# Latent attention beside the out-projection, regrouped from one head every four steps to two heads every eight

## The chip, the core and the metric

The kernel runs on one core of a Trainium2 chip. The metric is the device time of one execution in microseconds, the median of three runs. The profile is of one further execution; its times are in microseconds from the first instruction of the span.

## The reference, cut to what matters

One decoder layer over 256 tokens and 2048 channels, in float32: a pooling mixer, latent attention of 8 heads and cross attention of 4 heads to a memory run side by side, their outputs are joined and projected, and a gated feed-forward follows. The change touches the causal attention of the latent heads and its place beside the product with `w_o`:

```python
s = jnp.einsum('bqhd,bkhd->bhqk', qblk, k).astype(jnp.float32) * scale
s = jnp.where(mask[None, None], s, -jnp.inf)
pr = jax.nn.softmax(s, axis=-1).astype(v.dtype)
return jnp.einsum('bhqk,bkhd->bqhd', pr, v)
...
x = x + jnp.concatenate([y_pool, y_mla, y_mem], axis=-1) @ w_o[l]
```

## The kernel before

Every large product is done with operands split in two: a high part, a ScalarE cast (`split_w`, L103, tile `wh`), and a low part, a VectorE subtraction (L104, tile `wl`), and TensorE multiplies high by high, low by high and high by low (L185 to L187). Four pairs of `wh` and `wl` buffers rotate, so a cast waits until TensorE has finished with the buffer four casts earlier.

The out-projection is cut into parts. A part loads 128 x 2048 weights and does four **steps**: a step is one call of `gemm_n` with one row of weights, on two blocks of tokens with three products each, so 6 matmuls of 128 x 512. Two steps share one `wh`/`wl` pair. After each of the first 36 steps `mla_steps` is called, and `done[0]` counts these calls; "step 18" below is the place behind the 18th step. The first half of the input channels (pooling and memory heads) comes first; the latent heads are multiplied only in the second half, head 0 in step 33, head 4 in step 37, head 7 in step 40.

A latent head has three pieces of work on TensorE:

- `scores`: 6 matmuls into a bank of PSUM (`psa`), the last of each block of rows adds the causal mask (L823). Softmax follows on VectorE (L521, L522, L526, L528) and ScalarE (L524) and leaves the tile `p`.
- `turn`: three 128 x 128 transposes of `p` into a bank (L534), copied by ScalarE to `pT` (L537).
- `values`: two products of `pT` with the values (L542, L544) into a bank, whose 256 columns `split_act` turns into a high and a low part of `cat`: a ScalarE cast (L194) and a VectorE subtraction (L195), both reading the bank.

`psa` is a pool of four banks of 128 x 512 float32 that rotate. Head 0 and 1 have their scores at step 3. From step 6 on, every fourth step does `values` of head h-1, `turn` of head h and `scores` of head h+2, and step 36 does the last `values`. Matmuls and transposes in `keep(...)` stay in the order in which the code issues them; ScalarE and VectorE work and the matmuls after step 36 are placed by a scheduler when the program is built. Between them VectorE also prepares sums of the weights of the last product (`job_sums`, L610, tile `wk`) and adds finished sums to the residual (L886, tile `x1n`).

Of the kernel before, what the change touches and what calls it, by code (L numbers as in the profile page):

```python
# [18 lines left out]
P = 128  # L19
T = 256  # L20
# [3 lines left out]
H = 8  # L24
# [41 lines left out]
def layer(ctx, tc, xT_d, xn_d, memT_d, vec_d, tab_d, w_z_d, w_mqkr_d, w_q_d, w_kv_d, w_mem_d, w_pool_d, w_o_d,  # L66
          w_g_d, w_u_d, w_dn_d, out_d):
    nc = tc.nc
# [8 lines left out]
    def nm(s):  # L77
        uid[0] += 1
        return f"{s}_{uid[0]}"

    def ps_main():
        return psm.tile([P, 512], F32, tag="m", name=nm("psm"))

    def ps_aux():
        return psa.tile([P, 512], F32, tag="a", name=nm("psa"))
# [7 lines left out]
    def keep(ins, on=True):  # L93

        return tc.keep_in_program_order(ins) if on else ins
# [93 lines left out]
    def split_act(dst, src, scale=None, kept=False):  # L189


        h, l = (dst[:, 0], dst[:, 1]) if len(dst.shape) == 3 else (dst[:, 0:T], dst[:, T:2 * T])
        if scale is None:
            nc.scalar.copy(h, src)  # L194
            nc.vector.tensor_tensor(l, src, h.bitcast(F32), op=ALU.subtract)  # L195
        else:
            keep(nc.scalar.activation(h, src, AF.Copy, scale=scale), kept)
            keep(nc.vector.scalar_tensor_tensor(l, src, scale, h.bitcast(F32), op0=ALU.mult, op1=ALU.subtract), kept)
# [118 lines left out]
    ps = ps_aux()  # L317
# [40 lines left out]
    for c in range(KD // 2):  # L358
# [13 lines left out]
        if c % 2:  # L372
            h = slice(2 * c - 2, 2 * c + 2)
# [5 lines left out]
    ps = ps_aux()  # L379
# [126 lines left out]
    class Head:  # L506
# [5 lines left out]
            self.blocks = [(k, i) for k in range(2) for i, (a, b) in enumerate(spans) if b - a > k * P]  # L512

        def score(self):
            ps = ps_aux()
            self.scores(ps)
            p = self.p = mp.tile([P, 512], F32, tag="p", name=nm("p"), bufs=2)
            st = mp.tile([P, 8], F32, tag="st", name=nm("st"), bufs=4)
            n = len(self.spans)
            for i, (a, b) in enumerate(self.spans):  # L520
                nc.vector.tensor_reduce(st[:, i:i + 1], ps[:, a:b], axis=AX.X, op=ALU.max, negate=True)  # L521
            nc.vector.tensor_tensor(st[:, 2:2 + n], st[:, 0:n], self.f, op=ALU.mult)  # L522
            for i, (a, b) in enumerate(self.spans):
                nc.scalar.activation(p[:, a:b], ps[:, a:b], AF.Exp, bias=st[:, 2 + i:3 + i], scale=self.f[:, i:i + 1],  # L524
                                     accum_out=st[:, 4 + i:5 + i])
            nc.vector.reciprocal(st[:, 6:6 + n], st[:, 4:4 + n])  # L526
            for i, (a, b) in enumerate(self.spans):
                nc.vector.tensor_scalar(p[:, a:b], p[:, a:b], st[:, 6 + i:7 + i], None, op0=ALU.mult)  # L528
# [7 lines left out]
            nb = len(self.blocks) * P  # L536
            nc.scalar.copy(self.pT[:, :nb], tp[:, :nb])  # L537

        def values(self):
            nb = len(self.blocks) * P  # L540
            o = ps_aux()
            keep(nc.tensor.matmul(o[:, 0:T], self.v_of(0), self.pT[:, 0:T], start=True, stop=False,  # L542
                                  skip_group_check=True))
            keep(nc.tensor.matmul(o[:, 2 * T - nb:T] if nb < 2 * T else o[:, 0:T], self.v_of(1), self.pT[:, T:nb],  # L544
                                  start=False, stop=True, skip_group_check=True))
            split_act(self.dst, o[:, 0:T])

    class MemHead(Head):
# [70 lines left out]
    for m in range(6):  # L619
        raw = load_w(w_z_d[m], STG)  # L620
        ps = ps_main()[:, 0:T]
# [52 lines left out]
    def pool_out():  # L674
        for a in range(2):
            ps = ps_aux()
            for g in (2 * a, 2 * a + 1):
                keep(nc.tensor.matmul(ps[:, (g % 2) * T:(g % 2 + 1) * T], wp[:, g * P:(g + 1) * P], zp[:, g, :],
                                      start=True, stop=True))
            for g in (2 * a, 2 * a + 1):  # L680
                split_act(cat[:, g, :], ps[:, (g % 2) * T:(g % 2 + 1) * T], v("pool_scale", g))
# [119 lines left out]
    def rope_keys():  # L801
        for tt in range(NT):
            t = tok()
            nc.vector.tensor_tensor(t[:].rearrange("p (h d) -> p h d", d=ROPE), krr[:, tt].to_broadcast([P, H, ROPE]),
                                    fkr[:, tt * H:(tt + 1) * H].unsqueeze(2).to_broadcast([P, H, ROPE]), op=ALU.mult)
            ps = ps_aux()
            for i in range(4):
                nc.tensor.transpose(ps[:, i * P:(i + 1) * P], t[:, i * P:(i + 1) * P], identf[:])
            p3 = ps[:].rearrange("p (i t) -> p i t", t=P)
            k4 = krT.rearrange("p (i e) t -> p i e t", e=2)  # L810
            for e in range(2):
                r = slice(e * ROPE, (e + 1) * ROPE)
                nc.vector.tensor_copy(k4[r, :, e, tt * P:(tt + 1) * P], p3[r])


    def mla_head(h):
        def scores(ps):
            for tt, (a, n) in enumerate(((0, P), (P, 2 * P))):
                q = slice(tt * P, (tt + 1) * P)
                for l, r, o, b, e in ((qnT[:, h, q], knT[:, h, 0:n], a, True, False),  # L820
                                      (qrT[:, h // 2, q], krT[:, h, 0:n], a, False, False),
                                      (identb[:], cmask[:], a + n - P, False, True)):
                    keep(nc.tensor.matmul(ps[:, o:a + n], l, r, start=b, stop=e, skip_group_check=True))  # L823

        return Head(scores, ((0, P), (P, 3 * P)), fq3[:, :, h], lambda k: vv[:, k, h, :], cat[:, 4 + h, :])

    mla_heads = [mla_head(h) for h in range(H)]
    done = [0]

    def mla_steps():  # L830

        done[0] += 1
        if done[0] == 1:
            rope_keys()
        if done[0] == 3:
            pool_out()
            mla_heads[0].score()
            mla_heads[1].score()
        h, r = divmod(done[0] - 6, 4)
        if r == 0:  # L840
            if 0 < h < H:
                mla_heads[h - 1].values()
            if 0 <= h < H:
                mla_heads[h].turn()
            if 0 <= h < H - 2:
                mla_heads[h + 2].score()
        if done[0] == 4 * H + 4:
            mla_heads[H - 1].values()

    FIRST = (1, 3, 4, 6, 7, 9, 10, 12)  # L850

# [15 lines left out]
    def out_part(i, n, pss, c, o):  # L867

        raw = load_w(w_o_d[i, n, c], STG)
        for h in range(2):  # L870
            hi, lo = split_w(raw, h * HS, HS)
            w = [t.rearrange("p (k n) -> p k n", n=NN) for t in (hi, lo)]
            k = c * 4 + h * 2
            act, k = (cat, 4 + k) if i else (cat, k) if k < 4 else (catm, k - 4)
            for r in range(2):
                kept = i == 0 or n + c == 0
                gemm_n(pss, *(t[:, r:r + 1] for t in w), act, k + r, o + h + r == 0, o + h + r == 3, kept)
                if kept:
                    mla_steps()
        first_jobs()  # L880
# [8 lines left out]
    for n, c in ((0, 1), (1, 1), (0, 0), (1, 0), (2, 0), (2, 1), (3, 0), (3, 1)):  # L889
        begun = n in pss  # L890
# [118 lines left out]
    begun = len(FIRST)  # L1009
# [122 lines left out]
    done = None  # L1132
    for c in range(2):
# [23 lines left out]
        done = own  # L1157
# [85 lines left out]
```

## Time and profile before

| what | us |
|---|---|
| median of 3 runs (lowest, highest) | 986.72 (986.62, 986.81) |
| the profiled execution, whole | 987.05 |
| its span, first to last instruction | 985.3 |
| TensorE busy (PE) | 980.2 |
| VectorE busy (DVE) | 806.6 |
| ScalarE busy (ACT) | 580.9 |

PE is TensorE's matmul side, PEld its weight loads. The stage of the change lies between 180 and 250 us. A matmul's duration overlaps the next one, so the pace of TensorE is read from the starts of matmuls that follow each other, not from durations.

### The profile page before, as it was taken

How to read it: one execution, taken by the hardware profiler on the slowest of the kernel's cores; microseconds unless marked ns; L12 is line 12 of the kernel's file. 1: busy time of each engine (PE TensorE's matmuls, PEld its weight loads, DVE VectorE, ACT ScalarE, POOL GpSimd, SP SyncE). 2: the span in 40 equal slices, each digit the busy share in tenths (PEclk: the TensorE clock that was granted, in tenths of full speed). 3: DMA queues.
4: the chain of work that ended last, by engine and by line, in shares of the span. 5: the costliest groups of instructions: out<-in, count | busy, mean ns of one | idle time of the engine just before them, and what ended most of it. 6: DMA issues, size and time to landing. Idle time of an engine off the chain costs nothing.

```text
span 985.3 us, 17471 instructions
## 1 busy us (share of the span) xinstructions
PE 980.2 (99%) x6874; PEld 910.4 (92%) x6874; DVE 806.6 (82%) x1270; ACT 580.9 (59%) x805; POOL 70.3 (7%) x136
## 2 busy tenths in 40 slices
PE   9999999999999999999999999999999999999998
PEld 8899998888899999999999999999999888888886
DVE  6879689888767888787878877877777899999997
ACT  6778666544556554555455445555554677757773
POOL 1000000111100000000100100110000000000000
PEclk9999999999999999999999999999999999999999
DMA  9865556688967978987897988889897999999993
GB/s 359 314 224 197 207 198 244 241 314 301 362 246 294 348 268 294 333 298 283 316 337 268 317 284 309 323 303 339 297 361 277 329 396 378 396 347 391 393 394 128
DMA packets 51731, 300.67 MB, mean 305 GB/s; under 512 B 5824, under 2 KB 6336, under 8 KB 25920
## 3 DMA queue, kind: packets, MB, share of 16 engines
q1 hardware_dynamic: 33984, 214.73, 59.8%
q0 software_dynamic: 17232, 84.03, 22.6%
q8 instruction: 54, 0.88, 0.4%
q10 hardware_dynamic: 432, 0.79, 0.3%
q14 instruction: 29, 0.24, 0.1%
HBM read 259.28 MB, written 40.24 MB: 304 GB/s over the span
## 4 chain that ended last, share of the span: by engine, by line
PE 99%; DVE 0%; issue 0%
PE psm L169 48%; PE psm L185 5%; PE psm L187 5%; PE psm L186 5%; PE psm L150 4%; PE psa L1048 4%; PE psa L1047 4%; PE psa L1046 4%; PE psm L1048 4%; PE psm L1047 4%; PE psm L1046 4%; PE psm L134 3%; PE psa L823 1%; PE psa L185 1%; PE psa L187 1%; PE psa L186 1%
## 5 line engine op out<-in xcount | busy, mean ns | idle before, releaser
L104 DVE TENSOR_TENSOR wl<-wr,wh 128x1024 fp32r<-128x1024 f32 (+2 forms) x344 | 397.3, 1164 | 122.5 <-ACT wh L103 106.2
L103 ACT CAST wh<-wr 128x1024 fp32r<-128x1024 f32 (+2 forms) x344 | 343.2, 1005 | 177.3 <-PE psm L169 80.3
L169 PE MATMUL psm<-h,wh 128*128 128x256 f32 x2752 | 319.3, 276 | 0.0
L169 PEld LDWEIGHTS psm<-h,wh 128*128 128x128 f32 x2752 | 315.4, 188 | 0.0
L169 PE MATMUL psm<-h,wl 128*128 128x256 f32 x1376 | 163.1, 276 | 0.0
L169 PEld LDWEIGHTS psm<-h,wl 128*128 128x128 f32 x1376 | 159.3, 188 | 0.0
L956 ACT ACTIVATE gc<-psa,vec 128x256 f32<-128x256 f32 x44 | 24.9, 565 | 77.5 <-DVE psa L954 76.6
L610 DVE TENSOR_TENSOR wj<-wj 128x512 f32<-128x512 f32 x88 | 60.3, 686 | 1.1
L104 DVE TENSOR_TENSOR wl<-wj,wh 128x1024 fp32r<-128x1024 f32 (+1 forms) x50 | 53.7, 1092 | 4.8 <-PE psm L169 2.3
L103 ACT CAST wh<-wj 128x1024 fp32r<-128x1024 f32 (+1 forms) x50 | 47.1, 947 | 12.8 <-PE psm L1047 7.0
L959 ACT ACTIVATE gc<-gc 128x256 f32<-128x256 f32 x44 | 18.4, 418 | 55.3 <-DVE gc L958 55.3
L103 ACT CAST wh<-dn 128x1024 fp32r<-128x1024 f32 (+1 forms) x40 | 39.1, 988 | 19.5 <-DVE dn L1077 13.0
L104 DVE TENSOR_TENSOR wl<-dn,wh 128x1024 fp32r<-128x1024 f32 (+1 forms) x40 | 44.9, 1141 | 1.4 <-ACT wh L103 0.2
L958 DVE SCALAR_TENSOR_TENSOR gc<-psa,vec,gc 128x255 f32<-128x255 f32 x88 | 42.2, 479 | 1.5
L612 POOL DMA_DIRECT2D tsum<-wj x44 | 23.5, 534 | 212.0 <-DVE wj L610 188.7
L1048 PE MATMUL psm<-wl,aS 128*128 128x512 f32 x98 | 38.3, 391 | 0.0
L1048 PE MATMUL psa<-wl,aS 128*128 128x512 f32 x98 | 38.3, 391 | 0.0
L1047 PE MATMUL psm<-wh,aS 128*128 128x512 f32 x98 | 38.2, 390 | 0.0
L1047 PE MATMUL psa<-wh,aS 128*128 128x512 f32 x98 | 38.2, 390 | 0.0
L1046 PE MATMUL psm<-wh,aS 128*128 128x512 f32 x98 | 38.2, 390 | 0.0
L1046 PE MATMUL psa<-wh,aS 128*128 128x512 f32 x98 | 38.2, 390 | 0.0
L185 PE MATMUL psm<-wh,cat 128*128 128x512 f32 x96 | 38.1, 397 | 0.0
(282 smaller groups left out, 1479.9 us busy)
## 6 DMA issues: line engine op xcount, KB each, us to landing
wr<-in_w_g SPq DMA_DIRECT2D x44, 1024.0 KB, 6.9
wr<-in_w_u SPq DMA_DIRECT2D x44, 1024.0 KB, 7.4
wj<-in_w_dn POOLq DMA_DIRECT2D x22, 1024.0 KB, 7.5
tsum<-wj POOLq DMA_DIRECT2D x44, 512.0 KB, 7.1
wr<-in_w_o SPq DMA_DIRECT2D x16, 1024.0 KB, 6.4
wr<-tsum SPq DMA_DIRECT2D x15, 1024.0 KB, 7.9
wr<-in_w_dn SPq DMA_DIRECT2D x15, 768.0 KB, 7.8
wr<-in_w_z SPq DMA_DIRECT2D x10, 1024.0 KB, 4.9
```

Source lines behind the costliest of these rows:

```text
L103: keep(nc.scalar.copy(hi[:, c:e], raw[:, o + c:o + e]), kept)
L104: keep(nc.vector.tensor_tensor(lo[:, c:e], raw[:, o + c:o + e], hi[:, c:e].bitcast(F32), op=ALU.subtract), kept)
L150: keep(nc.tensor.matmul(ps, parts[k // nk][low][:, i * P:(i + 1) * P], m, start=k + a == 0 and low == low_first, stop=k == KD - 1 and low ...
L169: nc.tensor.matmul(ps, parts[k // nk][low][:, i * P:(i + 1) * P], m, start=k + a == 0 and low == (s == 1), stop=k == KD - 1 and low == (s ...
L185: keep(nc.tensor.matmul(ps, xh, hi[:, i, o], start=first and i == 0, stop=False), kept)
L186: keep(nc.tensor.matmul(ps, xl, hi[:, i, o], start=False, stop=False), kept)
L187: keep(nc.tensor.matmul(ps, xh, lo[:, i, o], start=False, stop=last and i == nk - 1), kept)
L610: keep(nc.vector.tensor_tensor(r[:, d], r[:, a], r[:, b], op=ALU.subtract))
L958: nc.vector.scalar_tensor_tensor(gc[:, d:T], g[:, 0:T - d], v(w, f), gc[:, d:T], op0=ALU.mult, op1=ALU.add)
L1046: nc.tensor.matmul(ps, a[0], b[0], start=first, stop=False)
L1047: nc.tensor.matmul(ps, a[1], b[0], start=False, stop=False)
L1048: nc.tensor.matmul(ps, a[0], b[1], start=False, stop=last)
```

## The change

`score` is cut into `begin` (the matmuls) and `soften` (the softmax). A table per piece of work says at which step which two heads have it. A group now does the values of two heads into the two halves of one PSUM bank, then the scores of two heads, then the transposes of two heads, at steps 10, 18, 26, and without new scores at 34; the last values come at step 36. Steps 6, 14, 22 and 30 have no attention work any more.

```diff
         def score(self):
-            ps = ps_aux()
-            self.scores(ps)
+            self.begin()
+            self.soften()
+
+        def begin(self):
+            self.ps = ps_aux()
+            self.scores(self.ps)
+
+        def soften(self):
+            ps = self.ps
...
-        def values(self):
-            nb = len(self.blocks) * P
-            o = ps_aux()
+        def values(self, o):
             keep(nc.tensor.matmul(o[:, 0:T], self.v_of(0), self.pT[:, 0:T], start=True, stop=False,
                                   skip_group_check=True))
-            keep(nc.tensor.matmul(o[:, 2 * T - nb:T] if nb < 2 * T else o[:, 0:T], self.v_of(1), self.pT[:, T:nb],
-                                  start=False, stop=True, skip_group_check=True))
+            keep(nc.tensor.matmul(o[:, P:T], self.v_of(1), self.pT[:, T:T + P], start=False, stop=True,
+                                  skip_group_check=True))
             split_act(self.dst, o[:, 0:T])
...
+    SCORES = {3: (0, 1), 10: (2, 3), 18: (4, 5), 26: (6, 7)}
+    TURNS = {10: (0, 1), 18: (2, 3), 26: (4, 5), 34: (6, 7)}
+    VALUES = {18: (0, 1), 26: (2, 3), 34: (4, 5), 36: (6, 7)}
...
-            mla_heads[0].score()
-            mla_heads[1].score()
-        h, r = divmod(done[0] - 6, 4)
-        if r == 0:
-            if 0 < h < H:
-                mla_heads[h - 1].values()
-            if 0 <= h < H:
-                mla_heads[h].turn()
-            if 0 <= h < H - 2:
-                mla_heads[h + 2].score()
-        if done[0] == 4 * H + 4:
-            mla_heads[H - 1].values()
+        if done[0] in VALUES:
+            o = ps_aux()
+            for e, h in enumerate(VALUES[done[0]]):
+                mla_heads[h].values(o[:, e * T:(e + 1) * T])
+        begun = [mla_heads[h] for h in SCORES.get(done[0], ())]
+        for head in begun:
+            head.begin()
+        for h in TURNS.get(done[0], ()):
+            mla_heads[h].turn()
+        for head in begun:
+            head.soften()
```

TensorE at step 18 before: the values of head 2 into `psa_342`, the transposes of head 3, then the scores of head 5 (the numbers tell buffers apart; the brackets name the engines waited for, Activation is ScalarE).

```order
L187 MATMUL psm_338_2367<-wl_341_2371,cat_1928 128x512
L542 MATMUL psa_342_2386<-pT_330_2321,vv_1402 128x256 [waits Activation_49]
L544 MATMUL psa_342_2386<-pT_330_2321,vv_1402 128x128
L534 MATMUL psa_343_2391<-identf_76,p_321_2266 128x128 [waits DVE_49,PE_49]
L534 MATMUL psa_343_2391<-identf_76,p_321_2266 128x128 [waits DVE_49]
L534 MATMUL psa_343_2391<-identf_76,p_321_2266 128x128
L823 MATMUL psa_345_2397<-qkv_1400 128x128 [waits DVE_49]
```

The same step now, with the values of heads 0 and 1 in one bank, `psa_335` (L547, L549 are the former L542, L544; L828 is L823).

```order
L187 MATMUL psm_331_2334<-wl_334_2338,cat_1928 128x512
L547 MATMUL psa_335_2353<-pT_315_2243,vv_1402 128x256 [waits Activation_49]
L549 MATMUL psa_335_2353<-pT_315_2243,vv_1402 128x128
L547 MATMUL psa_335_2353<-pT_317_2249,vv_1402 128x256 [waits DVE_49]
L549 MATMUL psa_335_2353<-pT_317_2249,vv_1402 128x128
L828 MATMUL psa_336_2362<-qkv_1400 128x128 [waits PE_49]
```

The second head's first product stands behind a wait for VectorE that no values product had before.

VectorE around that step before, from the adds to the residual on: the low part of head 2 (L195) stands behind one weight split.

```order
L886 TENSOR_TENSOR x1n<-x1n,psm_2164 128x512 [waits PE_49]
L528 TENSOR_SCALAR p_2330<-p_2330,st_2331 128x128 [waits DVE_49]
L528 TENSOR_SCALAR p_2330<-p_2330,st_2331 128x256
L104 TENSOR_TENSOR wl_2485<-wr_2438,wh_2484 128x1024 [waits Activation_49]
L104 TENSOR_TENSOR wl_2507<-wr_2504,wh_2506 128x1024 [waits DMAHW7_49,PE_49,Activation_49]
L195 TENSOR_TENSOR cat<-psa_2386,cat 128x256 [waits Activation_49]
```

VectorE now, around steps 18 and 26: both steps have their own rows here, cut where the softmax of step 18 stands.

```order
L893 TENSOR_TENSOR x1n<-x1n,psm_2164 128x512 [waits PE_49]
L615 TENSOR_TENSOR wk_2205<-wk_2205 128x512 [waits DVE_49]
L104 TENSOR_TENSOR wl_2451<-wr_2432,wh_2450 128x1024 [waits Activation_49]
L615 TENSOR_TENSOR wk_2205<-wk_2205 128x512 [waits DVE_49]
L104 TENSOR_TENSOR wl_2473<-wr_2470,wh_2472 128x1024 [waits DMAHW7_49,PE_49,Activation_49]
L195 TENSOR_TENSOR cat<-psa_2353,cat 128x256 [waits Activation_49] x2
...
L893 TENSOR_TENSOR x1n<-x1n,psm_2334 128x512 [waits PE_49]
L615 TENSOR_TENSOR wk_2329<-wk_2329 128x512 [waits DVE_49]
L104 TENSOR_TENSOR wl_2586<-wr_2567,wh_2585 128x1024 [waits Activation_49]
L615 TENSOR_TENSOR wk_2430<-wk_2430 128x512 [waits DMASW2_49,DMASW1_49,DMASW0_49]
L615 TENSOR_TENSOR wk_2430<-wk_2430 128x512 [waits DVE_49]
L195 TENSOR_TENSOR cat<-psa_2488,cat 128x256 [waits Activation_49]
```

At step 18 the subtraction of the first head stands behind a weight split, at step 26 behind one weight split and two sums that wait for no cast of that step.

TensorE at step 34 now: between the values of head 4 and of head 5 stand four matmuls of a later part (`psm_400`, `psm_401`), which the scheduler has put there.

```order
L547 MATMUL psa_384_2635<-pT_363_2515,vv_1402 128x256 [waits Activation_49]
L549 MATMUL psa_384_2635<-pT_363_2515,vv_1402 128x128
L185 MATMUL psm_400_2731<-wh_403_2735,cat_1928 128x512 [waits DVE_49,Activation_49]
L186 MATMUL psm_400_2731<-wh_403_2735,cat_1928 128x512
L185 MATMUL psm_401_2732<-wh_403_2735,cat_1928 128x512 [waits DVE_49]
L186 MATMUL psm_401_2732<-wh_403_2735,cat_1928 128x512
L547 MATMUL psa_384_2635<-pT_365_2521,vv_1402 128x256 [waits DVE_49]
L549 MATMUL psa_384_2635<-pT_365_2521,vv_1402 128x128
```

At step 36 nine matmuls of steps that follow stand in the same place, between the values of heads 6 and 7. The orders of GpSimd and of the DMA queue of SyncE are the same before and now.

## Rows read from the trace of the kernel before

**Rows 1.** The page, part 1: busy time, share of the span, instructions.
```profile
PE 980.2 (99%) x6874; PEld 910.4 (92%) x6874; DVE 806.6 (82%) x1270; ACT 580.9 (59%) x805; POOL 70.3 (7%) x136
```

**Rows 2.** The page, part 4: the chain that ended last, by engine.
```profile
PE 99%; DVE 0%; issue 0%
```

**Rows 3.** Busy by stretch: length, PE, PEld, DVE, ACT, POOL, PEclk, DMA share, GB/s.
```profile
182.00:250.00 68.00, 68.00 (x341) 56.99 (x340) 56.20 (x110) 33.72 (x68) 9.07 (x17) 1.00 0.81 295
```

**Rows 4.** Timeline, TensorE at step 18: start, duration, engine, line, out<-in, count.
```profile
210.18 0.39 PE L187 MATMUL psm<-wl,cat 128*128 128x512 f32 x1
210.41 0.59 PE L542 MATMUL psa<-pT,vv 128*128 128x256 f32 x2
210.84 0.38 PE L544 MATMUL psa<-pT,vv 128*128 128x128 f32 x2
211.06 0.49 PE L534 MATMUL psa<-identf,p 128*128 128x128 f32 x3
211.38 0.39 PE L823 MATMUL psa<-qkv 128*128 128x128 f32 x2
```

**Rows 5.** Timeline, TensorE: two scores in a row; a plain stretch; leaving a group.
```profile
181.13 0.22 PE L823 MATMUL psa<-cmask,identb 128*128 128x128 bf16 x1
181.19 0.44 PE L823 MATMUL psa<-qkv 128*128 128x128 f32 x2
...
223.62 0.39 PE L185 MATMUL psm<-wh,cat 128*128 128x512 f32 x1
...
226.34 0.59 PE L542 MATMUL psa<-pT,vv 128*128 128x256 f32 x2
...
228.74 0.22 PE L823 MATMUL psa<-cmask,identb 128*128 128x128 bf16 x1
228.77 0.48 PE L185 MATMUL psm<-wh,cat 128*128 128x512 f32 x1
229.08 0.40 PE L186 MATMUL psm<-wh,cat 128*128 128x512 f32 x1
```

**Rows 6.** Timeline at step 6: brackets hold idle time and what ended it.
```profile
186.65 0.39 PE L187 MATMUL psm<-wl,catm 128*128 128x512 f32 x1
186.91 0.46 PEld L534 LDWEIGHTS psa<-identf,p 128*128 128x128 f32 x3 [0.30 <-DVE p L528]
...
187.45 0.39 PE L823 MATMUL psa<-qkv 128*128 128x128 f32 x2
```

**Rows 7.** Timeline after step 3: VectorE and ScalarE on the pooling banks.
```profile
180.81 0.88 DVE L198 SCALAR_TENSOR_TENSOR cat<-psa,vec,cat 128x256 fp32r<-128x256 f32 x2
...
181.33 0.86 ACT L197 ACTIVATE cat<-psa,vec 128x256 fp32r<-128x256 f32 x2 [0.94 <-DVE cat L198]
```

**Rows 8.** Timeline at step 18: ScalarE and VectorE after the values.
```profile
210.42 1.04 ACT L103 CAST wh<-wr 128x1024 fp32r<-128x1024 f32 x1 [1.65 <-PE psm L186]
...
211.38 0.37 ACT L194 CAST cat<-psa 128x256 fp32r<-128x256 f32 x1
...
211.50 1.22 DVE L104 TENSOR_TENSOR wl<-wr,wh 128x1024 fp32r<-128x1024 f32 x1 [1.33 <-ACT wh L103]
...
212.64 0.42 DVE L195 TENSOR_TENSOR cat<-psa,cat 128x256 fp32r<-128x256 f32 x1
```

**Rows 9.** Timeline before step 26: the adds to the residual.
```profile
223.14 1.37 DVE L886 TENSOR_TENSOR x1n<-x1n,psm 128x512 f32<-128x512 f32 x2 [0.30 <-PE psm L187]
```

**Rows 10.** Timeline at step 34: VectorE's sums, the values, the low part.
```profile
240.31 2.13 DVE L610 TENSOR_TENSOR wk<-wk 128x512 f32<-128x512 f32 x3
240.77 0.59 PE L542 MATMUL psa<-pT,vv 128*128 128x256 f32 x2
...
242.36 0.42 DVE L195 TENSOR_TENSOR cat<-psa,cat 128x256 fp32r<-128x256 f32 x1
```

**Rows 11.** Timeline at step 10: the values and their low part.
```profile
194.47 0.59 PE L542 MATMUL psa<-pT,vv 128*128 128x256 f32 x2
...
196.86 0.41 DVE L195 TENSOR_TENSOR cat<-psa,cat 128x256 fp32r<-128x256 f32 x1
```

## The prediction

> **What bounds the kernel now.** I read the page's busy times first, then its chain, then the stretch of the change, then the timeline of one attention step. TensorE is busy for 980.2 of the 985.3 us [rows 1], and the chain that ended last is 99% TensorE, with nothing left for another engine [rows 2]. In the stretch from 182 to 250 us it is busy for all 68 us at a granted clock of 1.00 (2.4 GHz), while VectorE has 56 us and ScalarE 34 us [rows 3]. So anything that makes TensorE wait here is added to the end, and work taken off another engine gives nothing. In the timeline of step 18 the reader is to see that TensorE goes from the out-projection into values, transposes and scores without a gap: 0.23 us from the last matmul to the values, 0.65 us for the values of a head (210.41 to 211.06), 0.32 us for its three transposes [rows 4].
>
> **What the change removes.** The number of matmuls and transposes and their sizes stay the same: the second product of the values had 128 columns before, because a head has three blocks, and has 128 now. What goes are four visits, at steps 6, 14, 22 and 30. Entering one costs nothing (0.23 us, the pace of the out-projection: 12 matmuls from 223.62 to 226.34 are 2.72 us, 0.227 each [rows 5]). Leaving one costs 0.03 us to the first L185 and 0.31 us from there to the next matmul; staying among scores would have cost 0.06 and then an ordinary 0.227 [rows 5]. That is 0.34 against 0.29, 0.05 us per visit, 0.2 us for four.
>
> Step 6 has a wait of its own: its transposes start 0.26 us after the last out-projection matmul, and the scores 0.54 us after them, with VectorE's scaling of `p` as the releaser [rows 6]; 0.23 and 0.32 would be usual. That is 0.25 us. Head 0 is now turned at step 10, four steps later, so this wait goes, and nothing takes its place there: the scores of two heads stand before the transposes. Gains together: 0.45 us.
>
> **What the change adds: a wait between the two heads of one bank.** The values of two heads now share a bank, and between the two heads' products stand the ScalarE cast and the VectorE subtraction that read the first half. Does the second product wait for these readers? The order of the changed program says that it waits for VectorE. Its operand `pT` is ScalarE's; the VectorE work that has just been issued on this bank is the first head's subtraction. The trace of before shows how this program hands over a bank of which only half is concerned: after step 3 two results of the pooling mixer lie in one bank, and ScalarE's cast of the second pair (L197, 181.33) stood idle for 0.94 us until VectorE had finished its subtraction on the first pair (L198, 180.81) [rows 7]. These touch different columns. So I take it that a bank is handed over whole, and TensorE waits until L195 of the first head is done.
>
> The Trainium skill, page PSUM — Partial Sum Buffer, section "PSUM bank collisions raise a hardware error", speaks against this change in the same sense: PSUM is to be guarded by bank and 32-partition quadrant and not by address, since TensorE writing a bank while another engine reads other columns of it collides. By this rule the wait can't be left away, and the sum is the one below; if columns were guarded one by one, it would be the 0.45 us gain alone. Rows 7 agree with the rule, for two readers; no row of before has TensorE waiting in this way.
>
> **The price of the four waits.** I count from the start of the first head's values, t0. Unhindered, the second head's would start at t0 + 0.65 [rows 4]. A release passes in about 0.05 us: the weight cast ends at 211.46, the subtraction that needs it starts at 211.50 [rows 8].
>
> - Step 18. The queue is as in the step 18 of before: on ScalarE a weight cast that TensorE releases just at t0, then the cast of the values; on VectorE the weight subtraction that waits for that cast, then the values' subtraction. There L195 ended at 212.64 + 0.42 = 213.06, t0 + 2.65 [rows 8]. The second head starts at 2.70, that is 2.05 us late.
> - Step 26. On VectorE the two adds to the residual, one sum, a weight split, two sums, then L195. The adds of before ended 1.83 us ahead of such a step (223.14 + 1.37 = 224.51, against 226.34 [rows 5, 9]). A weight split takes 1.14 us to the next instruction (211.50 to 212.64 [rows 8]), a sum 0.68 (three from 240.31 to 242.36 [rows 10]). From t0 - 1.83 that gives 0.68 + 1.14 + 0.68 + 0.68 = 3.18, free at t0 + 1.35. The values' cast ends at 211.38 + 0.37, t0 + 1.34 [rows 8], so L195 runs from 1.40 to 1.82, and TensorE goes on at 1.87: 1.22 us late.
> - Step 34. The same queue as in the step 34 of before, three sums ahead of L195, which ended at 242.36 + 0.42 = 242.78, t0 + 2.01 [rows 10]. Here the scheduler has put four matmuls of a later part between the two heads. They need the weight cast that ends at t0 + 1.05 [rows 8], so they start at 1.10 and take 0.31 + 3 x 0.227 = 0.99, until 2.09. The second head starts there instead of at 0.65 + 4 x 0.227 = 1.56: 0.54 us late.
> - Step 36. Nine matmuls stand between: 0.65 + 0.31 + 8 x 0.227 = 2.78, and L195, behind one weight split as at step 18, is done at 2.65. It hides; 0.1 us stays for the extra leaving.
>
> Sum: 2.05 + 1.22 + 0.54 + 0.10 = 3.9 us of waits, less 0.45 us, gives **3.5 us slower**. The profiled execution took 987.05 us, 985.3 in the span and 1.75 around it; it would take 990.5. The median of before is 0.33 us lower than that execution, 986.72, so I predict **990.2 us**.
>
> Bounds. A wait at step 18 or 26 can't be shorter than the cast and the subtraction themselves, t0 + 1.87, that is 1.22 us each. At the other end, L195 came as late as t0 + 2.80 at step 10 (196.86 + 0.41 against 194.47 [rows 11]), and two sums ahead of it would make 4.17, a wait of 3.6 us. I take the positions that the order gives, with the durations of the matching steps; they are nearest to rows 8 and 10.
>
> What else could wait. The second head's transposes take the bank that the values used, so they wait for the second L195. From the second head's start to them are 0.65 us of values, two scores of 1.46 us each (at step 26 from 226.34 + 0.65 + 0.32 = 227.31 to 228.77 [rows 5]) and 0.33 us of transposes, 3.9 us; the cast and subtraction of that head need 1.8 us, and at step 26 one sum and one weight split (1.82 us) stand before. That fits. ScalarE gets bursts of two copies and four exponentials, but four weight buffers ahead cover several us, and VectorE and ScalarE have 12 and 34 us idle in the 68 [rows 3]; the wait itself gives them more.
>
> **The rivals.**
> - *No wait, so only the gain.* The VectorE wait could be for an old reader of that bank, done long ago. Then 986.72 - 0.45 = 986.3 us, not slower, within the 0.2% (2 us) that a measurement of this kernel tells from no change. For it: the order names only the engine. Against it: rows 7, and that no values product waited for VectorE before. It decides if the second L547 follows the first L549 by some 0.2 us. 5%.
> - *Short waits.* VectorE is idle for 1.33 us before the weight split at step 18 [rows 8]; if the values' subtraction found it free, steps 18 and 26 would cost 1.22 us each: 1.22 + 1.22 + 0.54 + 0.10 - 0.45 = 2.6, 989.3 us. Against it: VectorE works in order, and the weight split stands before. 15%.
> - *Long waits.* VectorE's softmax of two heads at once, or sums that wait for their transfers, run late into the next group. Then steps 18 and 26 cost 2.2 us each, as at step 10 of before (2.85 - 0.65 [rows 11]), step 34 2.85 - 1.56 = 1.3, step 36 0.1, less 0.45: 5.4, 992.1 us. For it: VectorE is busy for 83% of the stretch [rows 3]. 15%.
> - *The clock falls.* No row of before has TensorE idle for 2 us in mid run, and the clock stands at 1.00 [rows 3]. If it went to half (1.2 GHz) after each of the two long waits for some ten matmuls, 10 x 0.227 each would be added: 4.5 us more, 994.7 us. The Trainium skill, page TensorE: Matmul & The Clock Gate, Part 1, has the clock halved after idling; no run here shows it yet. 3%.
>
> **How the numbers follow.** The forecast itself, 3.2 to 4.3 us slower (989.9 to 991.0 us), has 62%. With the short and the long waits most of the chance lies between 988.9 and 992.4 us, which is the range; outside are the missing wait, the clock, and the tails. Slower by over 0.2% (above 988.7 us) are the forecast, the long waits, the clock and most of the short waits: 88%. Within 0.2%: the missing wait and what is left of the short ones, 9%. Faster 3%, for gains that I don't see.
>
> **What would show it.** At steps 18 and 26 an idle time of TensorE of about 2 and 1.2 us before the second L547, ended by L195 of VectorE; at step 34 a smaller one before the four matmuls, ended by the weight cast on ScalarE; none at 36. TensorE's busy time stays near 980 while the span grows to about 988.8. No idle time before the transposes of steps 10, 18 and 26. I am wrong if the second product follows the first at once, if the transposes wait too, or if the time is lost outside 180 to 255 us.

## Result, and the profile after

The changed kernel takes 992.30 us, the median of 6 runs (990.63 to 992.53); the kernel before took 986.76 beside it (986.62 to 987.11). The ratio is 1.005 (95% interval 1.004 to 1.0061): slower, as forecast, but by 5.5 us instead of 3.5. Its executions come in two groups, near 990.8 us with a mean granted clock of 0.999 to 1.000, and near 992.4 us with 0.998; the profiled execution, 990.63 us, is of the lower group, and the second group is the part that the forecast missed.

The page of the changed kernel: span, busy times, and the engines' shares of the chain that ended last.

```profile
span 988.9 us, 17473 instructions
...
PE 980.1 (99%) x6874; PEld 909.7 (92%) x6874; DVE 807.4 (82%) x1270; ACT 581.1 (59%) x805; POOL 70.1 (7%) x136
...
PE 97%; DVE 1%; ACT 1%; DMA 0%; issue 0%; ACTq 0%
```

TensorE does the same 980 us of work as in [rows 1], the span is 3.6 us longer, and VectorE and ScalarE have come into the chain, where they had nothing [rows 2]. The stretch of [rows 3] after (length, PE, PEld, DVE, ACT, POOL, PEclk, DMA share, GB/s), and TensorE's waits in it (total, times, longest):

```profile
182.00:250.00 68.00, 64.60 (x323) 53.96 (x322) 52.26 (x104) 32.76 (x66) 9.03 (x17) 1.00 0.80 279
```

```profile
PE psa L547 <- DVE cat L195: 3.1, 2, 1.9
...
PE psm L185 <- ACT wh L103: 0.3, 1, 0.3
```

The 3.4 us of idle time in the stretch are these three waits: two of a second head's values (L547) for the first head's subtraction (L195), one of the four matmuls at step 34 for their weight cast. The granted clock stayed at 1.00 in this execution. Step 18 in the timeline (start, duration, engine, line, out<-in; the bracket holds idle time and what ended it):

```profile
206.87 0.59 PE L547 MATMUL psa<-pT,vv 128*128 128x256 f32 x2
206.89 1.04 ACT L103 CAST wh<-wr 128x1024 fp32r<-128x1024 f32 x1 [1.65 <-PE psm L186]
...
207.84 0.36 ACT L194 CAST cat<-psa 128x256 fp32r<-128x256 f32 x1
207.97 1.23 DVE L104 TENSOR_TENSOR wl<-wr,wh 128x1024 fp32r<-128x1024 f32 x1 [0.59 <-ACT wh L103]
209.11 0.42 DVE L195 TENSOR_TENSOR cat<-psa,cat 128x256 fp32r<-128x256 f32 x1
...
209.58 0.70 PE L547 MATMUL psa<-pT,vv 128*128 128x256 f32 x2 [1.90 <-DVE cat L195]
...
210.34 0.39 PE L828 MATMUL psa<-qkv 128*128 128x128 f32 x2
```

The queue is that of [rows 8], moved 3.5 us earlier: weight cast, values' cast, weight split, subtraction. TensorE goes on 0.05 us after the subtraction's end. Steps 26, 34 and 36 likewise:

```profile
224.91 0.59 PE L547 MATMUL psa<-pT,vv 128*128 128x256 f32 x2
...
226.45 0.42 DVE L195 TENSOR_TENSOR cat<-psa,cat 128x256 fp32r<-128x256 f32 x1
...
226.92 0.70 PE L547 MATMUL psa<-pT,vv 128*128 128x256 f32 x2 [1.20 <-DVE cat L195]
...
242.28 0.59 PE L547 MATMUL psa<-pT,vv 128*128 128x256 f32 x2
...
243.39 0.50 PE L185 MATMUL psm<-wh,cat 128*128 128x512 f32 x1 [0.30 <-ACT wh L103]
...
244.43 0.61 PE L547 MATMUL psa<-pT,vv 128*128 128x256 f32 x2
...
248.52 0.59 PE L547 MATMUL psa<-pT,vv 128*128 128x256 f32 x2
...
251.26 0.68 PE L547 MATMUL psa<-pT,vv 128*128 128x256 f32 x2
```

From the first head's values to the second's are 2.71, 2.01, 2.15 and 2.74 us; the forecast had 2.70, 1.87, 2.09 and 2.78. For the net effect I compare the same two matmuls in both kernels: the first L185 after step 3, and the first transpose of the new residual behind the out-projection. Before:

```profile
182.69 0.48 PE L185 MATMUL psm<-wh,catm 128*128 128x512 f32 x1
...
261.55 1.04 PE L919 MATMUL psa<-identf,x1n 128*128 128x128 f32 x8
```

After:

```profile
182.66 0.48 PE L185 MATMUL psm<-wh,catm 128*128 128x512 f32 x1
...
265.43 1.03 PE L926 MATMUL psa<-identf,x1n 128*128 128x128 f32 x8
```

That is 78.86 and 82.77 us, 3.9 us more; 0.3 us come back behind it, up to the end of the span.

### The profile page after: what moved, and what is told of

It reads as the page before. It is cut to its first block, busy times and chain, and to the rows that moved or that the text cites. A ratio compares the mean times of both kernels' runs of the same rounds, so it can differ in the third digit from the quotient of the medians.

```text
span 988.9 us, 17473 instructions
## 1 busy us (share of the span) xinstructions
PE 980.1 (99%) x6874; PEld 909.7 (92%) x6874; DVE 807.4 (82%) x1270; ACT 581.1 (59%) x805; POOL 70.1 (7%) x136
## 4 chain that ended last, share of the span: by engine, by line
PE 97%; DVE 1%; ACT 1%; DMA 0%; issue 0%; ACTq 0%
PE psm L169 47%; PE psm L185 5%; PE psm L186 5%; PE psm L187 5%; PE psm L150 4%; PE psa L1055 4%; PE psa L1053 4%; PE psa L1054 4%; PE psm L1055 4%; PE psm L1053 4%; PE psm L1054 4%; PE psm L134 3%; PE psa L828 1%; PE psa L185 1%; PE psa L187 1%; PE psa L186 1%
## 5 line engine op out<-in xcount | busy, mean ns | idle before, releaser
L185 PE MATMUL psm<-wh,cat 128*128 128x512 f32 x96 | 38.3, 399 | 0.3 <-ACT wh L103 0.3
L186 PE MATMUL psm<-wh,cat 128*128 128x512 f32 x96 | 37.4, 389 | 0.0
```

The lines of the kernel that those rows point to most:

```text
L185: keep(nc.tensor.matmul(ps, xh, hi[:, i, o], start=first and i == 0, stop=False), kept)
L186: keep(nc.tensor.matmul(ps, xl, hi[:, i, o], start=False, stop=False), kept)
```

## The experiments

"Kernel 2" below is the kernel of experiment 2, and so on. Beside kernels 1 to 4, 5 to 8, 9 and 10, 11 and 12 the kernel before had medians of 987.12, 987.07, 987.06 and 986.98 us. The ratios, with their 95% intervals, lie near those of the means of all executions, so where executions fall into groups they differ from the ratio of the medians. "Group" means executions of one kernel that lie together.

### 1. The changed kernel once more

No edit; its use is a second profile.

> The changed kernel once more, nothing edited. The hand-over of the bank explains 3.6 us of a slow-down whose median was 5.5 us; the rest came in four of six executions, near 992.4 us, with a mean granted clock of 0.998 where the two others had 0.999 and 1.000 near 990.8 us. If a lowered clock is the second part, times come in two groups about 1.7 us apart, and a profile taken in the upper group shows a stretch at half clock behind one of the two long waits (steps 18 and 26). Rival: the second part is spread over the kernel (slower transfers), and no stretch stands out.

Measured: 992.24 us (990.84, 991.04, 992.24, 992.41, 992.59), ratio 1.0047 (1.0035 to 1.0059). The profile is of 992.59 us, the upper group. Its waits at steps 18 and 26 are 1.89 and 1.20 us, the same as before. What differs stands in the windows behind the wait of step 18 (length, PE busy, PEclk, DMA share, GB/s):

```profile
209.00:210.00 1.00, 0.12 (x1) 1.00 0.81 332
210.00:211.00 1.00, 1.00 (x8) 1.00 1.09 397
211.00:212.00 1.00, 1.00 (x7) 0.69 0.98 393
212.00:213.00 1.00, 1.00 (x5) 0.50 1.04 434
213.00:214.00 1.00, 1.00 (x7) 0.50 0.99 414
214.00:215.00 1.00, 1.00 (x4) 0.60 0.66 266
215.00:216.00 1.00, 1.00 (x10) 1.00 0.26 107
```

The granted clock drops from 1.00 to 0.50 (from 2.4 to 1.2 GHz) some 1.5 us after TensorE has resumed, and returns about 3.4 us later. The first score of step 18 starts at 210.63, the transposes at 215.31:

```profile
210.63 0.39 PE L828 MATMUL psa<-qkv 128*128 128x128 f32 x2
...
215.31 0.83 PE L541 MATMUL psa<-identf,p 128*128 128x128 f32 x6
```

4.68 us for what takes 3.01 in the lower group (210.34 to 213.35): 1.67 us more, near the distance of the two groups' means (992.4 less 990.9). Behind the 1.20 us wait at step 26 the clock stayed at 1.00. The theory holds: with the executions of the section above, 7 of 11 are of the upper group.

### 2. A bank for each head

```diff
-            o = ps_aux()
-            for e, h in enumerate(VALUES[done[0]]):
-                mla_heads[h].values(o[:, e * T:(e + 1) * T])
+            for h in VALUES[done[0]]:
+                mla_heads[h].values(ps_aux()[:, 0:T])
```

> Same groups of two heads, but the values of each head go to a bank of their own. Theory (hand-over of one bank between the two products): no idle time of TensorE in the stretch, 986.3 us, 0.45 us under before. Rival (two heads at once burden VectorE and ScalarE, and the bank is not the cause): stays at 990 to 992 us.

Measured: 987.28 us (986.51 to 988.12, 11 runs), ratio 1.0002 (0.9993 to 1.0011). No L547 waits any more, and the 5 us are gone with the shared bank, so the rival falls. The theory's time, 986.3 us, is missed by 1.0 us. 0.6 us of waits are left: the transposes of step 26 take the banks of the values and wait twice for a subtraction. That subtraction was late because VectorE's sums waited for a transfer of weights (`wk` from `in_w_dn`):

```profile
225.57 1.42 DVE L615 TENSOR_TENSOR wk<-wk 128x512 f32<-128x512 f32 x2 [2.62 <-DMA wk<-in_w_dn]
226.91 0.42 DVE L195 TENSOR_TENSOR cat<-psa,cat 128x256 fp32r<-128x256 f32 x1
```

### 3. One bank, both products ahead of its readers

```diff
-            split_act(self.dst, o[:, 0:T])
+            self.o = o
+        def spread(self):
+            split_act(self.dst, self.o[:, 0:T])
...
+            for h in VALUES[done[0]]:
+                mla_heads[h].spread()
```

> Still one bank for both heads, but the products of both heads are issued before the casts and subtractions that read the bank. Theory (the wait is for readers that stand between the two products): no wait before the second head's values, 986.3 us. Rival (sharing a bank costs by itself, for instance in TensorE's writes): stays above 988 us.

Measured: 988.32 us (986.19 to 991.16, 12 runs), ratio 1.0011 (1.0003 to 1.002). The profiled execution took 986.88 us and has no L547 wait: sharing the bank costs nothing there as long as no reader stands between the two writers. But the times spread over 5 us, which neither theory had, and the median lies where the rival had it; that the bank is not the reason follows from the four executions at 986.19 to 986.88 and from kernels 5 and 6. I put that down to head 7's subtraction at step 36, which stood behind a sum that waited 2.43 us for its transfer; kernels 5 and 6 show that this was wrong.

### 4. One bank at step 18 alone

```diff
-            o = ps_aux()
+            shared = ps_aux() if done[0] == 18 else None
```

> One bank at step 18 alone, two banks at steps 26, 34 and 36. Theory: one wait of 2.05 us, less the gain of 0.45 us: 988.3 us. If the longest wait alone brings the lower clock, some executions come about 1.7 us later still, near 990.0 us; if it takes the second wait at step 26 as well, all stay at 988.3 us.

Measured: 988.62 us (11 runs), ratio 1.0017 (1.0009 to 1.0026). Nine lie at 988.42 to 988.97 with a clock of 1.0, two at 990.00 and 990.45 with 0.998. The profile, of a lower one, has the wait of 1.9 us. So the wait of 1.9 us, less the gain, makes 1.5 us, and the two executions with the lower clock stand 1.4 and 1.8 us higher; with this wait as the only one the clock fell in 2 of 11. The theory holds.

### 5 and 6. Readers last with own banks at step 36; readers last once more

Kernel 5, over kernel 3 (kernel 6 is kernel 3 unchanged):

```diff
-            o = ps_aux()
+            o = ps_aux() if done[0] < 36 else None
...
+                last = done[0] == 36
+                mla_heads[h].values(ps_aux()[:, 0:T] if last else o[:, e * T:(e + 1) * T])
+                if last:
+                    mla_heads[h].spread()
```

> The changed kernel, but at steps 18, 26 and 34 both heads' products stand ahead of the casts and subtractions that read the shared bank, and at step 36 each head has a bank of its own and is read at once. Theory: the scatter of the kernel with the readers last (986.2 to 991.2 us) comes from head 7's low part, which stood on VectorE behind a sum of weights that waits for its transfer. Here both low parts of step 36 stand ahead of that sum, so the times lie close together, within 1 us, near the kernel before less the gain of 0.45 us (986.3 to 987.0 us), and TensorE has no wait of over 0.5 us between 180 and 255 us. Rival: the scatter comes from something else (the transfers, the clock); then the times spread over 3 us or more again.

> The kernel with the readers last at all four steps, run once more to have another profile. Theory: in an execution above 988 us TensorE stands before a product of head 7 (the low part of head 7's channels is late, its subtraction behind the sum of weights that waits for a transfer) for about as long as the time is above 986.5 us. If the profiled execution is one of the short ones, the wait is 0.3 us or less, as in the first profile. Rival: in a long execution the idle time or the lower clock is elsewhere.

Measured: kernel 5 988.28 us (986.13 to 990.02, 12 runs; five at 986.13 to 986.31, six at 988.23 to 989.17, one at 990.02), ratio 1.0006 (0.9997 to 1.0014). Kernel 6 990.02 us (986.14 to 990.48, 8 runs), ratio 1.0018 (1.0009 to 1.0028). The scatter stays without the queue at step 36: theory fallen. Both profiles are of high executions and show the place, step 26. Kernel 5, VectorE and TensorE:

```profile
225.65 1.42 DVE L618 TENSOR_TENSOR wk<-wk 128x512 f32<-128x512 f32 x2 [2.61 <-DMA wk<-in_w_dn]
226.98 1.22 DVE L104 TENSOR_TENSOR wl<-wr,wh 128x1024 fp32r<-128x1024 f32 x1
228.12 0.42 DVE L195 TENSOR_TENSOR cat<-psa,cat 128x256 fp32r<-128x256 f32 x1
...
228.98 0.42 DVE L195 TENSOR_TENSOR cat<-psa,cat 128x256 fp32r<-128x256 f32 x1
```

```profile
227.04 0.50 PE L541 MATMUL psa<-identf,p 128*128 128x128 f32 x3
...
229.54 0.52 PE L541 MATMUL psa<-identf,p 128*128 128x128 f32 x3 [2.00 <-DVE st L529]
```

The sums stand ahead of both subtractions on VectorE. Where their transfer lands late, everything behind them is late, and the second three transposes wait 2.0 us (2.2 in kernel 6; the profile names L529, but the second subtraction, which frees the bank, ended 0.06 us before it). Then the clock fell here too: to a mean of 0.66 between 230 and 235 us in kernel 5 and 0.68 in kernel 6. The sum is right: 986.2 + 2.0 + 1.7 = 989.9 for 990.02, and 986.14 + 2.2 + 1.7 = 990.0 for the 990.21 of kernel 6's profile. The executions at 988.2 to 988.6 would fit such a wait with the clock kept; no trace shows one. The sum does not cover all: two executions of kernel 6, at 989.88 and 990.16 us, have a mean clock of 1.000 and 0.999, so something else made them long, and it is not known what.

### 7. One bank at step 26 alone

```diff
-            o = ps_aux()
+            shared = ps_aux() if done[0] == 26 else None
```

> One bank for two heads at step 26 alone, at the other three steps a bank for each head. The wait of 1.2 us at step 26 stays, the one of 1.9 us at step 18 goes. Theory: 1.2 us over the two-bank kernel less what it saves, so 0.8 to 1.2 us over the kernel before (987.9 to 988.3 us), and a wait as short as this does not bring the granted clock down: no execution stands some 1.7 us above the others. Rival: the clock falls behind this wait as well; then some executions, 2 of 11 as with step 18 alone, stand 1.7 us higher with a mean clock of 0.998.

Measured: 991.68 us (987.95 to 993.96, 7 runs), ratio 1.0036 (1.0019 to 1.0054). Three executions at 987.95 to 988.41 are the theory; four at 991.68 to 993.96, with a clock of 0.996 to 0.998, are neither the theory nor its rival. The profile (992.59 us):

```profile
226.11 1.42 DVE L615 TENSOR_TENSOR wk<-wk 128x512 f32<-128x512 f32 x2 [2.82 <-DMA wk<-in_w_dn]
227.45 0.42 DVE L195 TENSOR_TENSOR cat<-psa,cat 128x256 fp32r<-128x256 f32 x1
...
227.92 0.84 PE L547 MATMUL psa<-pT,vv 128*128 128x256 f32 x2 [4.11 <-DVE cat L195]
```

The wait at step 26 is 4.1 us here, for the same late transfer (it landed at 226.0 us), and the clock falls behind it, to 0.50 between 229 and 231 us. In the two profiles of the changed kernel VectorE does not wait for it: the stall at step 18 brings these sums to 225.12 and 227.10 us, and the transfer had landed at 222.8 and 223.0. Take away the first wait, and the second grows in some executions.

### 8. The wait of step 18 made longer

Over kernel 4, `values` with four copies of the first half behind its subtraction:

```diff
+            spare = tok() if readers else None
+            for _ in range(readers):
+                nc.vector.tensor_copy(spare[:, 0:T], o[:, 0:T])
```

> One bank at step 18 alone, and behind the first head's subtraction VectorE copies the first half of the bank four more times (copies that nobody uses), so that the second head's product waits longer, about 3.2 us instead of 1.9. Theory: 1.3 us over the kernel with step 18 alone, 989.9 us, in executions without the lower clock; the longer idle time makes the fall to half clock more frequent, in half of the executions or more, which then take 1.7 us more, 991.6 us. Rival: whether the clock falls does not hang on the length of this wait (it is the other waits behind it, or chance); then it falls in 2 of 11 or fewer, as with step 18 alone.

Measured: 992.29 us (991.99 to 993.18, 5 runs), ratio 1.0055 (1.0042 to 1.0068). The four copies took 1.79 us, so the wait is 3.69 us, 1.8 more than in kernel 4. All five executions have a clock of 0.997 or 0.998. 988.62 + 1.8 + 1.7 = 992.1: the theory holds, with the half clock in 5 of 5 instead of 2 of 11; two of the five lie 0.9 us above the others, which is not explained. The profile at the wait's end (columns as in experiment 1):

```profile
211.00:212.00 1.00, 0.25 (x1) 1.00 1.01 373
212.00:213.00 1.00, 1.00 (x6) 0.62 0.99 414
213.00:214.00 1.00, 1.00 (x6) 0.50 0.96 401
214.00:215.00 1.00, 1.00 (x3) 0.50 0.60 246
215.00:216.00 1.00, 1.00 (x6) 0.67 0.24 98
```

### 9 and 10. The sums of two jobs one part later, in kernel 5 and in the kernel before

```diff
-    FIRST = (1, 3, 4, 6, 7, 9, 10, 12)
+    FIRST = (1, 3, 4, 7, 8, 9, 10, 12)
```

> The kernel with the readers last and own banks at step 36, and the weight sums of the fourth and fifth job issued one part (four steps) later, their transfers left where they were (the sixth job's transfer begins one part later with it). So no sum that may wait for a transfer stands on VectorE ahead of the subtractions of steps 26 and 34. Theory: the high executions of the kernel with readers last (988 to 990.5 us) come from such a sum at step 26, whose transfer was late by 2.6 us, and from the half clock behind that wait. Without it the times lie close together at 986.1 to 986.6 us, 0.5 to 0.9 us below the kernel before, and TensorE has no wait over 0.5 us between 180 and 255 us. Rival: the late transfer moves the wait elsewhere (another sum, a weight split); then the times still spread over 2 us or more.

> The kernel before, with the same two jobs of weight sums issued one part later. Theory: the kernel before has no wait at these sums, so its time stays at 987.1 us within 0.3 us, and what the regrouped kernel gains over it comes from the regrouping. Rival: the kernel before gains as well, 0.5 us or more; then the gain is that of the sums.

Measured: kernel 9 990.45 us (989.99 to 992.10, 5 runs), ratio 1.0035 (1.0023 to 1.0048); kernel 10 990.13 us (989.31 to 991.78, 10 runs), ratio 1.0032 (1.0022 to 1.0041). Both theories fell. Step 26 is clean in kernel 9: TensorE has no wait between 182 and 250 us, and the two marks of the section above stand at 182.99 and 261.35, 78.36 us apart. But a job's sums also free the buffer of a transfer to come, so one transfer, the seventh job's, went out at 254 us instead of 240, and sums wait further on; kernel 9, then kernel 10:

```profile
262.52 2.15 DVE L618 TENSOR_TENSOR wk<-wk 128x512 f32<-128x512 f32 x3 [4.28 <-DMA wk<-in_w_dn]
```

```profile
265.45 0.69 DVE L610 TENSOR_TENSOR wk<-wk 128x512 f32<-128x512 f32 x1 [7.05 <-DMA wk<-in_w_dn]
```

In kernel 10 TensorE then waits 1.9 us for a weight split, and the clock is 0.83 between 270 and 280 us; in kernel 9 it waits 0.9 and 0.4 us near 293 and 296, which is less than half of the 3.4 us that it loses behind the second mark against the kernel before; the rest is not explained. The kernel before hangs on the same transfers; its own order just meets them.

### 11 and 12. One transfer earlier, in kernel 5 and in the kernel before

```diff
-    FIRST = (1, 3, 4, 6, 7, 9, 10, 12)
+    FIRST = (1, 2, 4, 6, 7, 9, 10, 12)
```

> The kernel with the readers last and own banks at step 36, with one job of weight sums (the second) issued one part earlier, so that the transfer whose sums stand at step 26 is issued about 8 us earlier (at 196 instead of 204 us). Everything at step 26 keeps its place. Theory: the sum at step 26 no longer waits for its transfer, the transposes of step 26 no longer wait for VectorE (2.0 us in the profile before this one), and the high executions go: 986.1 to 987.0 us, close together. Rival: the earlier transfer makes another one late (a weight row of the out-projection, the sums of step 34); then 988 to 991 us or a wide spread stays.

> The kernel before with the same transfer issued one part earlier. Theory: no wait hangs on it there, 987.1 us within 0.3 us; the difference to the regrouped kernel with the same edit is what the regrouping gains without its waits, 0.2 to 0.9 us. Rival: it changes by 0.5 us or more either way, and the gain is one of transfers.

Measured: kernel 11 989.29 us (986.04 to 992.62, 12 runs), ratio 1.002 (1.0007 to 1.0033); kernel 12 987.08 us (986.59 to 987.39, 11 runs), ratio 1.0 (0.9992 to 1.0009). Five executions of kernel 11 lie at 986.04 to 986.72, seven at 988.73 to 992.62 (six of them with a clock of 0.998), so the scatter stays and its theory fell; that of kernel 12 holds. The edit did little, and it aimed at the wrong transfer: the one that it moves, to 203.53 us from 204.15 in kernel 5, feeds the four sums before those that stand at step 26. Between 195 and 262 us such transfers landed 5.1 to 9.6 us after they were issued (the first profile of the changed kernel, kernels 5 and 11), so none of 204 us is awaited at 225. The sums at step 26 use the next one, which goes out when the sums two jobs earlier have been stored (a job is one transfer and its four sums). Kernel 5, then kernel 11:

```profile
218.35 0.53 POOL L611 DMA_DIRECT2D wk<-in_w_dn  x1 [10.16 <-DMA tsum<-wk]
```

```profile
215.44 0.54 POOL L611 DMA_DIRECT2D wk<-in_w_dn  x1 [7.31 <-DMA tsum<-wk]
```

It landed 7.2 and 5.1 us later, at 225.6 and 220.5. Where it went out 1.4 us or more ahead of the row of `w_o` issued next to it (the first profile of the changed kernel, and kernels 1, 4, 8 and 11), it took 5.1 to 5.5 us; where it went out less than that ahead, or behind the row (kernels 2, 3, 5, 6 and 7), 6.5 to 8.9 us. So the two transfers, 1024 KB each, probably delay each other; no run moves one of them alone.

The profile of kernel 11 is of a low execution (986.22 us). Its step 26 is the counterpart to kernel 5's:

```profile
222.88 1.41 DVE L618 TENSOR_TENSOR wk<-wk 128x512 f32<-128x512 f32 x2
...
226.98 0.83 PE L541 MATMUL psa<-identf,p 128*128 128x128 f32 x6
```

No wait for the transfer, and six transposes in one go. Its marks:

```profile
182.58 0.48 PE L185 MATMUL psm<-wh,catm 128*128 128x512 f32 x1
...
260.94 1.03 PE L934 MATMUL psa<-identf,x1n 128*128 128x128 f32 x8
```

78.36 us, as in kernel 9: the regrouping without waits saves 0.50 us of the 78.86. Over the whole span this execution is 0.9 us shorter than the profiled one of the kernel before (984.4 against 985.3); the other 0.4 us lie outside the marks, and no run shows their cause. No version's median lies below that of the kernel before.

## Why the prediction was right, and where it was not

- **The wait between the two heads of a bank: right.** Kernel 2 (own banks) and kernel 3 (no reader between the writers) take it away, each alone. So it is the bank, handed over whole although the columns differ: TensorE waited 1.90 and 1.20 us for a reader of the other half. This wait is part of the program (the order has it ahead of the second head's product), and no run left it out, so what the chip would do without it is not shown. The Trainium skill, PSUM — Partial Sum Buffer, section "PSUM bank collisions raise a hardware error", asks for such a wait, by bank and not by address, and the program keeps to that. The rival without a wait (986.3 us) is refuted.
- **The size of the four waits: right within 0.15 us each.** Late by 2.06, 1.36, 0.59 and 0.05 us (the distances above less 0.65, 0.65, 1.56 and 2.69), 4.06 together, against 3.9. Step 26 lost 0.14 more than forecast, because the two sums ahead of the subtraction began 0.2 us after the values. After a wait the second head's values themselves take 0.11 us longer (209.58 to 210.34 is 0.76, not 0.65), at two steps; that was not in the sum. Short waits and long waits, as rivals, are both refuted for the changed kernel.
- **The gain: right.** 0.45 forecast, 0.50 measured between the marks on kernels 9 and 11. 4.06 + 0.22 - 0.50 gives 3.8; between the marks it is 3.9, over the span 3.6, in the forecast 3.5. "TensorE's busy time stays near 980 while the span grows to about 988.8" came out as 980.1 and 988.9.
- **The clock: the term that was mis-sized.** The step that failed is the rival "the clock falls", at 3% and 4.5 us, from half clock "after each of the two long waits for some ten matmuls". It happens after one of the two, costs 1.7 us, and in 7 of 11 executions, so it decides the median, 992.30 us: the upper group's mean is 992.4, the lower one's 990.9. The median lies in the range (988.9 to 992.4 us) by 0.1 us, and by luck: the long waits, at 992.1 us, had set that end, and they did not come, while the forecast had the clock outside the range. I had no row of before with such a wait, and gave the case a small chance for that reason alone; no row spoke against it either. The profiles show 0.50 for about 3.4 us behind waits of 1.89, 2.0, 2.2, 3.7 and 4.1 us, but 1.00 throughout behind two others of 1.9 (the first profile of the changed kernel, and kernel 4). The page cited for it (the Trainium skill, TensorE: Matmul & The Clock Gate, Part 1) has the clock halved after idling; the trace agrees on the halving. That page ties it to longer idling than waits of 1.9 to 2.2 us; here the measurement decides.
- **"That fits", of the transposes and the sums: right for the changed kernel, for a reason that I did not see.** Nothing waits there, since the stall at step 18 has VectorE reach the sums 2 us later, and their transfer took 5.1 us in both profiles. In kernels 4 and 8, which keep that stall, it had landed in time too. In kernels 2, 5, 6 and 7, without it, the transfer was late in the profiled execution; by their times it is so in about half of the executions of kernel 5, and perhaps of kernel 11, of which no trace shows a long one.

Open: why the clock falls in 7 of 11 executions of the changed kernel, but in 2 of 11 of kernel 4, with the same wait at the same place (11 executions each may also be chance); and what makes the stores of the sums, and with them the next transfer, early in one execution and late in the next.

## What to carry to other kernels

Packing two results into one PSUM bank cost nothing here where both were written before anything read the bank; a reader between the two writers put its whole queue on TensorE's path. On an engine that is busy 99% of the time a wait of some 2 us can cost nearly twice its length, so price such a wait with and without the half clock behind it. And before a wait is removed or moved, look at which transfers it had been hiding.

## What the runs showed of the hardware that I had not expected

- The fall to half clock lasts about 3.4 us and costs 1.7 us, and it does not begin at a fixed distance from the wait: some 1.5 us after TensorE resumed in experiment 1 (a wait of 1.89 us), some 0.5 us in experiment 8 (3.69 us); both from the share of half clock in the window where it falls.
- The transfer of the sums at step 26 waits for a store of earlier sums, which took 7.3 to 10.1 us to land; it went out between 215.4 and 218.4 us and took 5.1 to 8.9 us itself (the first profile of the changed kernel, and kernels 1 to 8 and 11). VectorE, which reaches these sums at about 223 us without the stall at step 18, found it landed in kernels 3 and 11 and waited until 225.6 to 226.1 in kernels 2, 5, 6 and 7. The DMA engines were busy for 0.91 to 0.99 of the time from 220 to 230 us in kernels 5 and 6.
